# Second pass of the attention scores' main key blocks with 64 rows, two blocks in the two row halves of the array

## The chip, the cores and the metric

One core of one Trainium2 chip runs the whole layer as a single program. The metric is the device time of one execution in microseconds (us): 1670.31 us, the median of three runs (1669.04 to 1671.41). Rows of the trace come from one profiled execution. PE is TensorE, the matrix engine; PEld is its loading of weights, the operand that stays in the array; DVE is VectorE, ACT is ScalarE, POOL is GpSimd, and SP is the engine whose queue issues all transfers (DMAs).

## The reference, cut to what matters

One layer of a hybrid block: a normalised input is projected once, then a gated linear attention and a differential attention run on it, and both are merged, projected and added to the input. The change touches the scores of the differential attention alone: 8 heads, 1024 queries in 8 tiles of 128, 1280 keys (256 of the context, 1024 of the latents), and two components per head, each of width 64.

```
s1 = jnp.einsum('bhqd,bhkd->bhqk', qb1, k1).astype(jnp.float32) * scale
s2 = jnp.einsum('bhqd,bhkd->bhqk', qb2, k2).astype(jnp.float32) * scale
a = jax.nn.softmax(s1, axis=-1) - lam * jax.nn.softmax(s2, axis=-1)
return jnp.einsum('bhqk,bhkv->bhqv', a.astype(v.dtype), v)
```

## The kernel before

**Products in two parts.** The kernel works in float32 and has PE multiply in fp32r, a faster and less exact form. To keep the precision it splits an operand into a high part and a low part. Elsewhere a product takes three matmuls (high by high, high by low, low by high: `mm3`, line 359). For the scores the width is only 64, so both parts of the keys lie in one tile of 128 rows: `kk`, rows 0 to 63 the high part, rows 64 to 127 the low part (lines 1918 to 1920, two loads of 64 x 1280 from `d_kT[0]` and `d_kT[1]`). The query tile `aq` holds the same part of the queries in both row halves, index 0 the high part and index 1 the low part. So a first matmul over 128 rows gives high query by (high + low) key, and a second one adds low query by (high + low) key into the same place.

**One unit of scores** is one query tile of one head (`att_scores`, line 1957). Its output `s5` is one PSUM region of 2560 columns, 5 banks of 512. For each component two main blocks of 512 keys go to two banks of their own (`MAIN`, line 2050), and the remaining 256 keys of both components share the middle bank (`TAIL`, line 2049). Each block takes the two matmuls described above, so a unit is eight matmuls of 512 columns and four of 256, and there are 64 units. After a component's main blocks DVE takes the maximum over 1024 columns (`att_max`), ACT takes the exponential over 1280 columns out of PSUM (`att_exp`), DVE combines the two components (`att_mix`), PE transposes the result (`att_tr`; tiles `b` from `ident` and `e`), ACT and POOL split it into two parts, and PE multiplies it by the values (`att_av`; `b` from `at` and `vv`).

**What sets the order.** Every engine runs its instructions in the order written into the program. A planner (`Driver`, line 57) writes that order when the program is built: it keeps a clock for PE (`now`), prices every instruction by formulas (`mm`, line 353, prices a matmul of 512 columns at 0.009 + 512 x 0.000428 = 0.228 us), and lets the task with the highest priority go whose inputs are due by that clock. A `yield AtPE(0)` gives other tasks a turn. Between the attention's matmuls it places matmuls of the output gates and of the branch projections (`fill`, line 2215; tile `mb` from `h` and `wt`), spread over the units by `PACE` (line 2123). The last of them need the finished attention and come after it.

**Buffers of the keys.** `kk` has three buffers. A head uses two, the third already holds the first component of the next head, and the second component's load waits until the current head's last use of a buffer. SP issues transfers strictly in its own order, and waits for what a transfer needs.

Of the kernel before, what the change touches and what calls it, by code (L numbers as in the profile page):

```python
# [19 lines left out]
P = 128  # L20
# [3 lines left out]
T = S + CTX  # L24
# [221 lines left out]
class Hybrid:  # L246
# [22 lines left out]
        mm=("psA", 2), ma=("psA", 1), tp=("psA", 2), edge=("sbE", 1), gs=("psA1", 1), go=("psA1", 1), gt=("psA1", 1),  # L269
# [80 lines left out]
            yield  # L350
        self.d.spawn(later(), AtPE(at), prio=-9)

    def mm(self, out, lhsT, rhs, start, stop, more=False):
        self.ins = self.nc.tensor.matmul(out, lhsT, rhs, start=start, stop=stop, skip_group_check=more).ins  # L354
        n = rhs.free_size()
        c = 0.009 + max(n, 230) * 0.000428 if rhs.dtype == F32R else 0.006 + max(4 * n, 470) / 2400
        return self.d.op("PE", c, [out], [lhsT, rhs])

    def mm3(self, out, sh, sl, mh, ml, first, last, more=False):
        self.mm(out, sh, mh, first, False, more)  # L360
# [1544 lines left out]
    def att_keys(self):  # L1905

        yield self.ev_us
        for hd in range(8):
            c, x = hd // 4, hd % 4
            for i in range(10):  # L1910
                yield self.ev_st["dk", c, i]
            if hd:
                yield self.ev_q[0, 1]
            K = []
            for comp in range(2):
                rows = slice(64 * comp, 64 * comp + 64)
                yield from self.acq("kk")
                kt = self.t("kk", [P, T], F32R)
                self.dma(kt[0:64], self.d_kT[0][c][x, rows])
                self.dma(kt[64:128], self.d_kT[1][c][x, rows])  # L1920
                K.append(kt)
            self.K[hd] = K
            self.d.set(self.ev_k[hd], self.d.when(*K))
# [33 lines left out]
    def att_scores(self):  # L1957

        nc, d = self.nc, self.d
        yield self.ev_b  # L1960
        s5 = self.t("s5", [P, 2 * T])
        for hd in range(8):
            for qt in range(8):
                pr, qs = qt // 2, slice((qt % 2) * P, (qt % 2) * P + P)
                yield self.ev_k[hd]
                yield self.ev_q[hd, pr]
                K, Q = self.K[hd], self.Q[hd, pr]

                def score(po, comp, o, n):
                    bank = po.offset % (2 * T) // 512  # L1970
                    for j in range(2):
                        e = self.mm(po, Q[comp][:, j, qs], K[comp][:, o:o + n], j == 0, j == 1)
                        self.banked(self.ins, "PE", bank)
                    return e

                if qt % 4 == 0:
                    self.zs = self.t("sm", [P, 4, 2])
                u = dict(hd=hd, qt=qt, E=[None, None], mt=self.t("sm", [P, 2]), mx=[self.t("sm", [P, 1]) for _ in range(2)],
                         z=self.zs[:, qt % 4], zs=self.zs, left=2, min=[], ev=[Event() for _ in range(3)])

                for comp in range(2):
                    yield from self.acq(f"s{comp}")
                    pm = s5[:, 1536 * comp:1536 * comp + 1024]
                    for x, (o, n) in enumerate(self.MAIN[comp]):
                        e = score(pm[:, x * 512:(x + 1) * 512], comp, o, n)
                        if x == 0:
                            yield AtPE(0)
                    d.spawn(self.att_max(u, comp, s5, pm, 3 * comp, 3 * comp + 1), On(e, "DVE"), prio=-3)
                    yield AtPE(0)
                    if comp == 0:  # L1990
                        yield from self.acq("st")
                        pt = s5[:, 1024:1536].rearrange("p (c k) -> p c k", c=2)
                        for x in range(2):
                            e = score(pt[:, x], x, *self.TAIL[x])
                        d.spawn(self.att_max(u, 2, s5, pt, 2), On(e, "DVE"), prio=-3)
                    elif qt == 7:
                        self.rel("kk", e, 2)
                    yield AtPE(0)
                if qt % 2 == 1:
                    self.rel("aq", e, 2)  # L2000
                d.set(self.ev_u[8 * hd + qt])
# [47 lines left out]
    TAIL = ((1024, 256), (0, 256))  # L2049
    MAIN = (((0, 512), (512, 512)), ((256, 512), (768, 512)))  # L2050
    GROUPS = ((0, 4), (4, 4), (8, 2))

    def att_tr(self):

        d = self.d
        for hd in range(8):
            for qt in range(8):
                x = qt % 2
                yield self.ev_a[hd, qt]
                E = self.att[hd, qt][0]  # L2060
                if x == 0:
                    A = self.aT[hd, qt // 2] = []
                for g, (k0, n) in enumerate(self.GROUPS):
                    if x == 0:
                        tg = "at4" if n == 4 else "at2"
                        yield from self.acq(tg, 2)
                        A.append([self.t(tg, [P, n, 2, P], F32R) for _ in range(2)] + [tg])
                    if n == 2 and x == 0:
                        E0 = E
                        continue  # L2070
                    hi, lo = A[g][:2]
                    tb = "mc" if "psC" in self.pools else "b1"
                    yield from self.acq(tb)
                    if n == 4:
                        pt = self.t(tb, [P, n, P])
                        for j in range(n):
                            e = self.tr(pt[:, j], E[:, (k0 + j) * P:(k0 + j + 1) * P])
                        d.spawn(self.att_split(g, pt, hi[:, :, x], lo[:, :, x], [self.ev_aT[hd, qt, g]], tb), On(e, "ACT"), prio=self.PS)
                    else:
                        pt = self.t(tb, [P, 2, 2, P])  # L2080
                        for j in range(2):
                            for y, EE in enumerate((E0, E)):
                                e = self.tr(pt[:, j, y], EE[:, (k0 + j) * P:(k0 + j + 1) * P])
                        d.spawn(self.att_split(g, pt.rearrange("p a b t -> p (a b) t"), hi.rearrange("p a b t -> p (a b) t"),
                                               lo.rearrange("p a b t -> p (a b) t"),
                                               [self.ev_aT[hd, qt - y, g] for y in range(2)], tb), On(e, "ACT"), prio=self.PS)
                    yield AtPE(0)
                if x:
                    self.rel("e5", e, 2)

    def att_av(self):
        d = self.d
        for hd in range(8):
            for pr in range(4):
# [8 lines left out]
                VH, VL = self.V[hd]  # L2103
                for g, (k0, n) in enumerate(self.GROUPS):
                    hi, lo, tg = A[g]
# [583 lines left out]
```

## Time and profile before

| What | Value |
|---|---|
| median of three runs | 1670.31 us (1669.04 to 1671.41) |
| the profiled execution, its own time | 1671.82 us |
| its span, first to last instruction | 1670.1 us |
| PE busy | 1621.8 us, 97% of the span, 8317 matmuls |
| DVE busy | 1203.2 us, 72% |
| ACT busy | 832.1 us, 50% |
| POOL busy | 642.7 us, 38% |
| DMA | 178 GB/s on average |
| granted TensorE clock | 0.998 on average |

Matmuls overlap: the next one starts streaming while the one before still drains, so the recorded length of one is longer than the time it takes from the engine. The scores run from 970.7 us to about 1448 us of the span; after that come the end of the attention, the last branch projection and the output projection.

### The profile page before, as it was taken

How to read it: one execution, taken by the hardware profiler on the slowest of the kernel's cores; microseconds unless marked ns; L12 is line 12 of the kernel's file. 1: busy time of each engine (PE TensorE's matmuls, PEld its weight loads, DVE VectorE, ACT ScalarE, POOL GpSimd, SP SyncE). 2: the span in 40 equal slices, each digit the busy share in tenths (PEclk: the TensorE clock that was granted, in tenths of full speed). 3: DMA queues.
4: the chain of work that ended last, by engine and by line, in shares of the span. 5: the costliest groups of instructions: out<-in, count | busy, mean ns of one | idle time of the engine just before them, and what ended most of it. 6: DMA issues, size and time to landing. Idle time of an engine off the chain costs nothing.

```text
span 1670.1 us, 24453 instructions
## 1 busy us (share of the span) xinstructions
PE 1621.8 (97%) x8317; PEld 1344.4 (81%) x8317; DVE 1203.2 (72%) x1868; ACT 832.1 (50%) x1665; POOL 642.7 (38%) x619
## 2 busy tenths in 40 slices
PE   8999999999999999999999989999999999999999
PEld 3788888888788878888888778888888888878887
DVE  4675878878645475767777568897888888746694
ACT  4786568553523344442333346666666566642231
POOL 1600662643100113435454425555656566730000
PEclk9999999999999999999999999999999999999999
DMA  8646576455555464459999654443874534257422
GB/s 308 212 154 218 187 229 208 126 163 193 187 176 164 147 205 159 138 187 294 288 292 297 190 149 108 127 133 92 232 239 125 147 107 127 66 187 246 150 98 76
DMA packets 267005, 297.62 MB, mean 178 GB/s; under 512 B 23640, under 2 KB 186368, under 8 KB 266880
## 3 DMA queue, kind: packets, MB, share of 16 engines
q1 hardware_dynamic: 266880, 296.05, 56.8%
q8 instruction: 66, 1.08, 0.3%
q14 instruction: 59, 0.48, 0.1%
HBM read 196.37 MB, written 99.61 MB: 177 GB/s over the span
## 4 chain that ended last, share of the span: by engine, by line
PE 55%; DVE 10%; POOL 3%; issue 3%; ACT 3%; DMA 1%; SPq 0%; ACTq 0%; DVEq 0%; POOLq 0%
PE mc L354 10%; PE mm L354 7%; PE s L354 6%; PE mb L354 6%; PE b L354 5%; PE ma L354 5%; DVE sm L211 4%; PE go L354 3%; PE b L380 3%; PE gs L354 3%; PE gt L354 3%; PE tp L354 2%; DVE e L211 2%; ACT e L211 2%; POOL p L211 1%
## 5 line engine op out<-in xcount | busy, mean ns | idle before, releaser
L211 DVE TENSOR_REDUCE sm<-s 128x1 f32<-128x1024 f32 (+1 forms) x192 | 197.4, 1038 | 33.2 <-PE s L354 32.4
L354 PE MATMUL mm<-w,h 128*128 128x512 f32 x864 | 217.9, 400 | 3.3 <-DVE us L211 1.3
L211 ACT ACTIVATE e<-s,sm 128x1280 f32<-128x1280 f32 x128 | 170.1, 1331 | 86.4 <-DVE sm L211 78.3
L211 POOL TENSOR_TENSOR at<-ac,at 128x512 fp32r<-128x512 f32 x128 | 185.9, 1453 | 10.7
L354 PEld LDWEIGHTS mm<-w,h 128*128 128x128 f32 x864 | 158.8, 188 | 38.0 <-DVE us L211 1.7
L354 PE MATMUL s<-kk,aq 128*128 128x512 f32 (+1 forms) x768 | 174.1, 361 | 6.8 <-ACT e L211 6.8
L354 PE MATMUL mb<-h,wt 128*128 128x512 f32 x624 | 170.6, 404 | 6.1 <-DVE ft L211 3.6
L211 POOL TENSOR_SCALAR at<-ac 128x512 fp32r<-128x512 f32 x128 | 97.3, 760 | 188.5 <-ACT ac L211 183.2
L354 PE MATMUL mm<-h,w 128*128 128x512 f32 x624 | 154.1, 396 | 0.0
L354 PEld LDWEIGHTS s<-kk,aq 128*128 128x128 f32 x768 | 121.0, 188 | 26.3 <-ACT e L211 10.7
L354 PEld LDWEIGHTS mm<-h,w 128*128 128x128 f32 x624 | 115.6, 189 | 23.4 <-DVE h L211 0.2
L354 PE MATMUL b<-at,vv 128*128 128x256 f32 x960 | 129.7, 283 | 1.9 <-DVE at L211 1.5
L354 PEld LDWEIGHTS mb<-h,wt 128*128 128x128 f32 x624 | 109.6, 188 | 26.9 <-DVE ft L211 4.7
L354 PEld LDWEIGHTS b<-at,vv 128*128 128x128 f32 x960 | 120.9, 188 | 7.5 <-POOL at L211 2.7
L211 POOL TENSOR_TENSOR sm<-sm,nhalf 128x8 f32<-128x8 f32 (+3 forms) x78 | 103.1, 1322 | 30.9 <-DVE sm L211 25.6
L354 PE MATMUL mc<-h,wt 128*128 128x512 f32 x480 | 113.1, 396 | 1.6 <-DVE wt L211 1.6
L211 DVE SCALAR_TENSOR_TENSOR e<-e,sm,e 128x1280 f32<-128x1280 f32 x64 | 112.3, 1755 | 1.2
L354 PEld LDWEIGHTS mc<-h,wt 128*128 128x128 f32 x480 | 90.8, 190 | 22.3 <-DVE wt L211 2.5
L211 ACT ACTIVATE ac<-b 128x512 f32<-128x512 f32 x121 | 71.9, 598 | 57.3 <-PE b L380 55.0
L354 PE MATMUL ma<-w,h 128*128 128x512 f32 x384 | 96.8, 397 | 0.4 <-DVE gp L211 0.4
L380 PE MATMUL b<-ident,e 128*128 128x128 f32 x604 | 87.6, 273 | 6.8 <-DVE at L211 3.1
L380 PEld LDWEIGHTS b<-ident,e 128*128 128x128 f32 x604 | 72.5, 141 | 23.9 <-ACT ac L211 3.9
(385 smaller groups left out, 3170.2 us busy)
## 6 DMA issues: line engine op xcount, KB each, us to landing
raw<-in_w_in SPq DMA_DIRECT2D x37, 512.0 KB, 4.6
rb<-in_w_in SPq DMA_DIRECT2D x64, 256.0 KB, 2.9
aq<-d_qT SPq DMA_DIRECT2D x128, 128.0 KB, 4.0
d_kT<-pl SPq DMA_DIRECT2D x40, 256.0 KB, 2.4
d_dv<-pl SPq DMA_DIRECT2D x40, 256.0 KB, 2.3
kk<-d_kT SPq DMA_DIRECT2D x32, 320.0 KB, 5.2
gv<-d_v SPq DMA_DIRECT2D x40, 256.0 KB, 4.2
vv<-d_dv SPq DMA_DIRECT2D x16, 640.0 KB, 6.6
```

Of the source, the lines that this page charges most:

```text
L211: self.ins = f(out, *args, **kw).ins
L354: self.ins = self.nc.tensor.matmul(out, lhsT, rhs, start=start, stop=stop, skip_group_check=more).ins
L380: self.nc.tensor.transpose(out, src, self.ident[:n, :n])
```

## The change

In the second pass (low part of the queries) the two main blocks of a component are multiplied by the high part of the keys alone: 64 rows each instead of 128. The first block uses rows 0 to 63, the second block rows 64 to 127. So that both find the high part there, the halves of the key tile are swapped from the second block's first key on (`o`, 512 for the first component and 768 for the second): the load of a key tile becomes four transfers of 64 x 512 and 64 x 768 instead of two of 64 x 1280. What falls away is low query by low key in the main blocks. The four matmuls of a component now stand in the order first block high, second block high, first block low, second block low, without a turn for others between the blocks; the planner prices the two low ones at 0.1 and 0.23 us (`HALF`). The tail keeps both passes over 128 rows.

```diff
-    def mm(self, out, lhsT, rhs, start, stop, more=False):
+    def mm(self, out, lhsT, rhs, start, stop, more=False, cost=None):
...
-        return self.d.op("PE", c, [out], [lhsT, rhs])
+        return self.d.op("PE", cost or c, [out], [lhsT, rhs])
...
                 kt = self.t("kk", [P, T], F32R)
-                self.dma(kt[0:64], self.d_kT[0][c][x, rows])
-                self.dma(kt[64:128], self.d_kT[1][c][x, rows])
+                o = self.MAIN[comp][1][0]
+                for j, part in enumerate((slice(0, o), slice(o, T))):
+                    for hh in range(2):
+                        self.dma(kt[64 * hh:64 * hh + 64, part], self.d_kT[hh ^ j][c][x, rows, part])
...
-                def score(po, comp, o, n):
-                    bank = po.offset % (2 * T) // 512
-                    for j in range(2):
-                        e = self.mm(po, Q[comp][:, j, qs], K[comp][:, o:o + n], j == 0, j == 1)
-                        self.banked(self.ins, "PE", bank)
+                def score(po, comp, o, n, j, rows=slice(0, P), cost=None):
+                    e = self.mm(po, Q[comp][rows, j, qs], K[comp][rows, o:o + n], j == 0, j == 1, cost=cost)
+                    self.banked(self.ins, "PE", po.offset % (2 * T) // 512)
                     return e
...
                     for x, (o, n) in enumerate(self.MAIN[comp]):
-                        e = score(pm[:, x * 512:(x + 1) * 512], comp, o, n)
-                        if x == 0:
-                            yield AtPE(0)
+                        score(pm[:, x * 512:(x + 1) * 512], comp, o, n, 0)
+                    for x, (o, n) in enumerate(self.MAIN[comp]):
+                        e = score(pm[:, x * 512:(x + 1) * 512], comp, o, n, 1, slice(64 * x, 64 * x + 64), self.HALF[x])
...
                         for x in range(2):
-                            e = score(pt[:, x], x, *self.TAIL[x])
+                            for j in range(2):
+                                e = score(pt[:, x], x, *self.TAIL[x], j)
...
+    HALF = (0.1, 0.23)
```

On PE, one unit of the second head before. `s5` is the scores' region, `kk` a key tile, `aq` a query tile, `b1` a bank that takes transposes, `mb` a filler's bank; the size is that of the output, so the rows of the operands don't show here.

```order
L354 MATMUL s5_1958_9420<-kk_1939_9298,aq_2106_10105 128x512 x2
L380 MATMUL b1_2152_10305<-ident_207,ot_2108_10111 128x128 x2
L380 MATMUL b1_2152_10305<-ident_207,ot_2144_10286 128x128 x2
L354 MATMUL s5_1958_9420<-kk_1939_9298,aq_2106_10105 128x512 x2
L380 MATMUL b1_2153_10313<-ident_207,e5_2116_10136 128x128 x4
L354 MATMUL mb_2117_10138<-h0_150_640,wt_2046_9802 128x512
L354 MATMUL mb_2117_10138<-h0_151_641,wt_2046_9802 128x512
L354 MATMUL mb_2117_10138<-h0_150_640,wt_2047_9803 128x512
L354 MATMUL s5_1958_9420<-kk_1939_9298,aq_2106_10105 128x256 x2
L354 MATMUL s5_1958_9420<-kk_2072_9931,aq_2107_10108 128x256 x2
L354 MATMUL s5_1958_9420<-kk_2072_9931,aq_2107_10108 128x512 x4
```

The same unit of the same head after the change.

```order
L354 MATMUL s5_1956_9419<-kk_1939_9305,aq_2101_10082 128x512 x4
L354 MATMUL mb_2111_10131<-h0_150_640,wt_2043_9801 128x512
L354 MATMUL mb_2111_10131<-h0_151_641,wt_2043_9801 128x512
L354 MATMUL mb_2111_10131<-h0_150_640,wt_2044_9802 128x512
L354 MATMUL s5_1956_9419<-kk_1939_9305,aq_2101_10082 128x256 x2
L354 MATMUL s5_1956_9419<-kk_2058_9883,aq_2102_10085 128x256 x2
L354 MATMUL s5_1956_9419<-kk_2058_9883,aq_2102_10085 128x512 x4
L380 MATMUL b1_2154_10338<-ident_207,ot_2109_10127 128x128 x2
L380 MATMUL b1_2154_10338<-ident_207,ot_2149_10310 128x128 x2
```

The four matmuls of 512 columns always follow each other now (128 groups of four; before, 9 of the 128 had other work between the two blocks), and the other work in the unit has moved by a few rows; before the first key load, at PE's row 3208, the order is unchanged.

On SP, the key loads where the first head gives way to the second, before; `d_kT00` holds high parts, `d_kT10` low parts, and `d_m12` and `d_bT0` are other stores.

```order
L319 DMA d_m12_130<-ft_2045_9800 128x512
L319 DMA kk_2072_9931<-d_kT00_88 64x1280
L319 DMA kk_2072_9931<-d_kT10_90 64x1280
L319 DMA aq_2073_9934<-d_qT0_86 64x2x256 x2
L319 DMA aq_2074_9937<-d_qT0_86 64x2x256 x2
L319 DMA kk_2075_9940<-d_kT00_88 64x1280
L319 DMA kk_2075_9940<-d_kT10_90 64x1280
L319 DMA d_bT0_112<-b1k_2087_10013 128x512
```

The same place after the change.

```order
L319 DMA d_m12_130<-ft_2042_9799 128x512
L319 DMA kk_2058_9883<-d_kT00_88 64x768
L319 DMA kk_2058_9883<-d_kT10_90 64x768
L319 DMA kk_2058_9883<-d_kT10_90 64x512
L319 DMA kk_2058_9883<-d_kT00_88 64x512
L319 DMA aq_2059_9888<-d_qT0_86 64x2x256 x2
L319 DMA aq_2060_9891<-d_qT0_86 64x2x256 x2
L319 DMA kk_2061_9894<-d_kT00_88 64x512
L319 DMA kk_2061_9894<-d_kT10_90 64x512
L319 DMA kk_2061_9894<-d_kT10_90 64x768
L319 DMA kk_2061_9894<-d_kT00_88 64x768
```

Each key tile takes four issues instead of two, with the same bytes in all, and the query loads behind it stand two issues later.

## Rows read from the trace of the kernel before

**Rows 1.** Page, part 1: busy time, share of the span and instructions.
```profile
PE 1621.8 (97%) x8317; PEld 1344.4 (81%) x8317; DVE 1203.2 (72%) x1868; ACT 832.1 (50%) x1665; POOL 642.7 (38%) x619
```
**Rows 2.** Windows, scores and what follows: length, PE, PEld, DVE, ACT, POOL, clock, DMA.
```profile
970.70:1450.30 479.60, 460.40 (x2892) 400.74 (x2891) 406.93 (x614) 301.28 (x578) 284.01 (x251) 1.00 0.48 135
1450.30:1670.10 219.80, 213.42 (x997) 176.42 (x995) 140.24 (x213) 66.28 (x119) 22.65 (x21) 0.99 0.44 148
```
**Rows 3.** Chain that ended last, from 970 to 1450 us, shares by engine and line.
```profile
by line: PE s L354 21.7%; PE mb L354 16.4%; PE b L354 15.8%; DVE sm L211 12.3%; PE b L380 10.6%; DVE e L211 7.3%; ACT e L211 5.9%; issue 4.3%; DVE at L211 0.9%; POOL sm L211 0.8%; DVE b1k L211 0.8%; DMA aq<-d_qT 0.8%; ACT ac L211 0.8%; POOL
```
**Rows 4.** Waits, 970 to 1450 us: us in total, times, longest.
```profile
ACT e L211 <- DVE sm L211: 77.4, 51, 4.2
DVE sm L211 <- PE s L354: 32.4, 22, 13.4
PE s L354 <- ACT e L211: 6.8, 9, 2.8
PE mb L354 <- DVE ft L211: 3.6, 3, 1.8
PE b L380 <- DVE at L211: 3.1, 2, 1.5
```
**Rows 5.** Groups by shape, scores and transposes: busy, mean ns, idle before.
```profile
L354 PE MATMUL s<-kk,aq 128*128 128x512 f32 x512 | 143.6, 399 | 5.2 <-ACT e L211 5.2
L354 PE MATMUL s<-kk,aq 128*128 128x256 f32 x256 | 41.3, 283 | 1.6 <-ACT e L211 1.6
...
L380 PE MATMUL tp<-ident,p 128*128 128x128 f32 x144 | 21.9, 275 | 2.1 <-DVE p L211 1.1 <-POOL p L211 0.7
```
**Rows 6.** Chain in order of time: start, us, what; runs of 512 and 256 columns.
```profile
1027.50 2.83 PE b L354 x24
1612.03 21.76 PE mc L354 x96
```
**Rows 7.** Instructions on the scores' tile: duration ns min/median/max.
```profile
L354 PE MATMUL s<-kk,aq x768: 276/392/503, 970.7 to 1448.0; 128*128 128x512 f32 x128, 128*128 128x256 f32 x64
```
**Rows 8.** Timeline, PE and PEld near 24.6 us: two-row matmuls, then 128 rows.
```profile
24.41 0.40 PE L380 MATMUL gt<-ident,p 2*128 2x2 f32 x4 [0.63 <-DVE p L211]
24.62 0.20 PE L380 MATMUL gt<-ident,p 2*128 2x2 f32 x1
24.74 0.20 PEld L380 LDWEIGHTS tp<-ident,g 128*128 128x128 f32 x2
24.74 0.77 PE L380 MATMUL tp<-ident,g 128*128 128x128 f32 x5
24.91 0.14 PEld L380 LDWEIGHTS tp<-ident,g 128*128 128x128 f32 x1
```
**Rows 9.** Timeline, PE and PEld near 31.3 us: 128 columns of weights, then 4.
```profile
31.29 0.39 PE L354 MATMUL mm<-h,w 128*128 128x512 f32 x1
31.30 0.31 PEld L354 LDWEIGHTS gs<-w,cs 128*4 128x4 f32 x2
31.52 0.63 PE L354 MATMUL gs<-w,cs 128*4 128x512 f32 x2
```
**Rows 10.** DMA issues: count, KB each, median us to landing.
```profile
kk<-d_kT SPq DMA_DIRECT2D x32, 320.0 KB, 5.2
aq<-d_qT SPq DMA_DIRECT2D x128, 128.0 KB, 4.0
```
**Rows 11.** Timeline, SP's queue and PE where the second head ends.
```profile
1073.05 1.10 SPq L319 DMA_DIRECT2D kk<-d_kT  x2
1074.20 2.52 SPq L319 DMA_DIRECT2D aq<-d_qT  x4
1079.85 1.55 PE L354 MATMUL s<-kk,aq 128*128 128x512 f32 x8
```
**Rows 12.** Timeline, SP's queue before the linear attention.
```profile
761.70 0.45 SPq L319 DMA_DIRECT2D kk<-d_kT  x1
762.20 0.58 SPq L319 DMA_DIRECT2D bkt<-d_kt  x1
762.82 0.45 SPq L319 DMA_DIRECT2D gv<-d_v  x1
```

## The prediction

> **What bounds the kernel now.** I read the page's busy times first, then windows of the stage that changes, then the chain there, then the waits. PE is busy almost throughout, no other engine is [rows 1]; a busy PE is a modelled figure, so it only says where to look. In the stage of the scores, 479.6 us long, PE is the fullest engine and DVE the second with 406.9 us, 85% [rows 2]. So DVE would bound this stage only if it shrank by 73 us, far more than the change can take. The chain there runs through PE for about two thirds: the scores alone hold 21.7%, the fillers 16.4%, the products with the values 15.8%, the transposes 10.6%; DVE's maximum and mix and ACT's exponential hold 25.5% together [rows 3]. PE itself waits little: 6.8 us for the exponential that frees a scores' bank, 3.6 us and 3.1 us for DVE, while ACT and DVE wait for each other and for the scores far longer [rows 4]. The stage is therefore a full PE with about a third of the chain passing through the DVE and ACT loop. What follows is PE again: 213.4 of 219.8 us [rows 2], with the same fillers left over.
>
> **What a matmul takes.** A scores' matmul of 512 columns is recorded with 399 ns [rows 5], but they overlap. In a long run 96 matmuls of 512 columns take 21.76 us, so each takes 0.227 us from PE; 24 of 256 columns take 2.83 us, so 0.118 us [rows 6]. The scores thus take 512 x 0.227 + 256 x 0.118 = 146 us from PE.
>
> **The pair of half matmuls.** The change leaves the count at 12 matmuls per unit and makes four of them half as high. It makes 128 pairs (64 units, two components). A pair took 2 x 0.227 = 0.453 us. What it takes now no row of before shows: there is no matmul of 64 rows in this stage. The bounds:
> - Nothing is gained if the two run one after the other, each with all its columns: 0.453 us.
> - Everything is gained if they stream side by side: 0.227 us.
> - In between stands the weight load. Weights of a following matmul normally load while the one before streams, unseen. When they can't, the load shows: scores' matmuls have a median of 392 ns and a longest of 503 ns [rows 7], so an uncovered load of 128 columns costs 111 ns. The second half matmul's load stands behind the first half matmul in PE's order. If it starts only once that one has started, the second streams 0.111 us after the first, and the pair takes 0.111 + 0.227 = 0.338 us.
> I take the 0.338 us: the row that comes nearest is this load, and elsewhere a load begins when the matmul before it begins, not sooner (31.30 behind 31.29 us) [rows 9]. That saves 0.453 - 0.338 = 0.115 us a pair, 128 x 0.115 = 14.7 us of PE.
>
> The Trainium skill (TensorE: Matmul & The Clock Gate, Part 3) says that matmuls in distinct row groups start within 4 ns of each other, since the loads are pulled ahead. By that rule a pair would take 0.231 us. No row of before has two row groups, so it stays with the second rival.
>
> **What of it reaches the end.** The scores hold 21.7% of the chain over 480 us, so 104 us of their 146 us lie on it, 0.71. The rest of the time the chain passes through DVE and ACT, and a shorter matmul only lets PE wait longer. 14.7 x 0.71 = 10.5 us. What is late next is DVE's maximum of 1024 columns and ACT's exponential; both keep their lengths. The fillers don't run out: they are spread over the units, and those that are left after the scores are on PE anyway.
>
> **The key loads.** Sixteen key tiles take four issues instead of two, 32 more on SP. Two issues take 1.10 us [rows 11], so about 0.55 us each. Where a head ends, the second component's keys are issued at 1073.05 us and land 5.2 us after issue [rows 10], about 1078.8 us for the later one; the next head's scores start at 1079.85 us. The cover is 1 us. With four issues the last starts 1.1 us later; its piece is 128 or 192 KB instead of 320 KB, and query loads of 128 KB land in 4.0 us, so most of the delay comes back. I cost it at nothing. Without that cover it is at most 1.1 us at each of 7 changes of head, 7.7 us. Query loads stand behind them and are due two units later. Before the stage, the first head's keys stand ahead of loads for the linear attention [rows 12]; two more issues there are 0 to 1.1 us, I take 0.5.
>
> **The order.** Taking the turn between the blocks away costs nothing by itself, and only 9 of 128 groups had used it. But the planner's clock is 0.126 us shorter per pair, so from its first key load on the order of all engines is laid anew. A few matmuls of a filler more or less between two units is 0.7 us each time, in both directions; I count 0.5 us against the change and 3 us either way for the range.
>
> **Sum.** 10.5 - 0.5 - 0.5 = 9.5 us less. The profiled execution took 1671.82 us, 1.7 us more than its span, and 1.5 us more than the median; the same difference from the median 1670.31 gives 1660.8, so 1661 us.
>
> **Rivals.**
> - *The halves stream side by side.* The pair takes 0.227 us, PE saves 128 x 0.227 = 29 us, and at 0.71 and with the same 1 us against it the time is 1670.3 - 20.6 + 1 = 1651 us. For it: the operands lie in different rows and the results in different banks. Against it: a load starts with the matmul before it [rows 9].
> - *The change of height stops PE.* This is the one that makes it slower. Every pair needs two changes, from 128 rows to 64 and back. There is one place without a wait where matmuls of few rows are followed by 128 rows [rows 8]: four of two rows start 0.07 us apart, the last at 24.62 us, and the load for 128 rows starts only at 24.74 us, 0.12 us later, and it is seen: the next load starts at 24.91 us, 0.17 us after, where the remaining three of the five are (0.77 - 0.17 - 0.275) / 3 = 0.11 us apart (0.275 us is the mean length of such a transpose [rows 5]). Together 0.05 + 0.06 = 0.11 us lost. Twice that makes the pair 0.338 + 0.22 = 0.558 us, 0.105 us more than before, 13.4 us of PE; 0.71 to all of it on the path, with the 1 us, gives 1681 to 1685 us, 1683 us. It decides from 0.058 us a change on, half of the 0.115 us gained. The upper bound is that each change waits for the whole drain, 0.392 - 0.227 = 0.165 us, and then loads weights uncovered, 0.111 us: the pair takes 0.89 us, 128 x 0.437 = 56 us more, 1711 us at 0.71. Against it: weights of 4 columns follow 128 columns elsewhere, and the matmul starts 0.23 us later as always, with its load at the usual time [rows 9]; but there the rows stay the same.
> - *The halves run one after the other.* PE gains nothing, the order is laid for a gain that isn't there, and the loads cost their 1 us: 1670 to 1675 us, 1672 us. For it: each still streams 512 columns.
> - *The gain falls into the DVE and ACT loop.* If only 0.4 of the saved time reaches the end, 14.7 x 0.4 - 1 = 4.9 us are left, 1665 us. I count this within the forecast.
>
> The Trainium skill (TensorEngine Tiling (Array Packing), Key Properties) has a rule that speaks against the change: changing the tiling mode, not just the tile, drains the engine. The trace agrees by 0.11 us for a change in rows [rows 8], and shows no such loss for a change in columns [rows 9]. By the rule in full the time is that of the second rival's upper half.
>
> **Chances.** Forecast (0.338 us a pair) 0.42; side by side 0.14; stopped by the change of height 0.31; one after the other 0.13. The forecast's own range is 1655 to 1668 us: 0.4 to 0.9 of 14.7 us, less the 1 us, and 3 us either way for the order. The range of 8 in 10 reaches into both sides: 1651 us leaves out half of the side-by-side case, 0.07, and 1688 us leaves out a third of the stopped case, 0.11. A measurement tells about 0.2% (3.3 us) from no change. Faster by more: 0.40 of the forecast, all 0.14 of side by side, 0.01 of the rest: 0.55. Slower by more: 0.28 of the stopped case, 0.03 of one after the other: 0.31. Within: 0.14.
>
> **What the new profile would show.** Right: groups of 64 rows, 256 in all, the second of a pair starting about 0.11 us after the first and the next full matmul 0.23 us after that; the scores' stage some 10 us shorter with DVE's busy time in it unchanged at 407 us; PE's waits for the exponential a few us longer; the first scores of a head no later behind their key loads than the 6.8 us of now [rows 11]. Wrong: a gap of 0.1 us or more before the first half matmul or behind the second, with its weight load starting late (stopped); 0.227 us between the two (one after the other); nearly equal starts (side by side). If the pair takes 0.338 us and the time still doesn't fall by 6 us, the share of 0.71 was wrong; if SP's key loads end a wait of PE at the heads' ends, the cover of 1 us was.

## The result: 1690.5 us against 1670.9 us, slower by 1.2%

The changed kernel takes 1690.48 us (median of four runs, 1687.09 to 1693.42), the kernel before in the same session 1670.86 us (1669.04 to 1672.08). The ratio is 1.0118, its 95% interval 1.0096 to 1.014: 19.6 us lost where 9.5 us were to be won, and outside the range of 1651 to 1688 us. The profiled execution took 1689.76 us, with a span of 1688.0 us.

The page after, busy times; they answer to [rows 1].

```profile
PE 1642.5 (97%) x8317; PEld 1315.6 (78%) x8317; DVE 1204.6 (71%) x1867; ACT 831.4 (49%) x1665; POOL 641.3 (38%) x620
```

PE has as many instructions as before and 21 us more of (modelled) busy time; the busy time of its weight loads is 29 us less. A load of 64 rows is about as long as one of 128 (185 and 191 ns on average), but the two loads of a pair run at the same time, so 256 of them fill only 24.1 us. Every other engine does what it did.

The instructions on the scores' tile after: minimum, median and longest duration in ns, then the first and the last start in us; this answers to [rows 7].

```profile
L354 PE MATMUL s<-kk,aq x768: 275/397/794, 968.0 to 1468.4; 128*128 128x512 f32 x128, 128*128 128x256 f32 x64
```

The scores now take 500.4 us from first to last start, 23.1 us more than the 477.3 us before. They begin 2.7 us earlier and what follows them is 2.5 us shorter, so the stage holds the whole loss.

The chain that ended last, after, from 970 to 1450 us, for [rows 3].

```profile
by line: PE s L354 25.5%; PE mb L354 21.3%; PE b L354 20.1%; PE b L380 13.9%; DVE sm L211 5.4%; ACT e L211 2.6%; DVE e L211 2.3%; issue 1.8%; DMA aq<-d_qT 1.6%; POOL at L211 1.1%; DVE b1k L211 0.8%; DMA raw<-in_w_br_gla 0.8%; ACT ac L211 0.
```

PE's four lines hold 81% of it instead of 64.5%; DVE and ACT have fallen back. So PE became slower, and nobody else's waits took its place. The scores' groups by shape, 960 to 1480 us, for [rows 5] (busy us, mean ns of one, idle us just before them and what ended it), and two waits of the stage for [rows 4].

```profile
L354 PE MATMUL s<-kk,aq 128*128 128x512 f32 x256 | 83.5, 408 | 6.9 <-ACT e L211 6.9
...
L354 PE MATMUL s<-kk,aq 64*128 64x512 f32 x256 | 64.8, 503 | 0.0
...
L354 PEld LDWEIGHTS s<-kk,aq 64*128 64x128 f32 x256 | 24.1, 185 | 47.1 <-issue 47.1
```

```profile
PEld s L354 <- issue: 46.8, 131, 0.7
...
PE s L354 <- ACT e L211: 7.3, 8, 2.5
```

A half matmul is recorded with 503 ns on average, the length of a matmul whose weight load is not covered (before, the longest was 503 ns [rows 7]), and the loads for it stood idle 47.1 us with nothing in the trace to wait for. The timeline shows one pair: PE's matmuls and PEld's loads in order of start (start us, length us; in brackets the idle time before).

```profile
1037.88 0.39 PE L354 MATMUL s<-kk,aq 128*128 128x512 f32 x1
1038.10 0.40 PE L354 MATMUL s<-kk,aq 128*128 128x512 f32 x1
1038.43 0.19 PEld L354 LDWEIGHTS s<-kk,aq 64*128 64x128 f32 x2 [0.36 <-issue]
1038.43 0.50 PE L354 MATMUL s<-kk,aq 64*128 64x512 f32 x2
1038.86 0.30 PEld L354 LDWEIGHTS b<-at,vv 128*128 128x128 f32 x2 [0.25 <-issue]
1038.86 0.39 PE L354 MATMUL b<-at,vv 128*128 128x256 f32 x1
```

Both loads of the pair start 0.33 us behind the second full matmul, where the load before had started together with a matmul; the two half matmuls lie in one row of 0.50 us, that is, on top of each other; the next load, of 128 rows, again starts only 0.43 us later. Over the 128 pairs the medians of the starts are: from the second full matmul to the first half one 326 ns, to the second half one 3 ns, to what follows 429 ns. With full rows in the same order (the first experiment) each of the three is 232 ns. What follows is then seen with its own load as well: a matmul takes 107 to 114 ns more than with full rows (65 pairs), a transpose 56 ns more (63 pairs). Row by row against full rows, a pair loses 0.17 us of PE with a matmul behind it and 0.12 us with a transpose behind it, 18.7 us in all. The expectations below reckon 0.184 us behind every pair, 23.6 us; they count a matmul's load there each time and 0.227 us for a distance that is 0.232 us here, so they are some 5 us too high.

The key loads, for [rows 10] and [rows 11]: the issues by size (count, KB, median us to landing), and four of them in SP's queue.

```profile
kk<-d_kT SPq DMA_DIRECT2D x32, 192.0 KB, 3.4
kk<-d_kT SPq DMA_DIRECT2D x32, 128.0 KB, 3.6
```

```profile
1079.64 2.38 SPq L319 DMA_DIRECT2D kk<-d_kT  x4
```

Four issues take 2.38 us, 0.6 us each, and their pieces land 1.6 to 1.8 us sooner than the whole did.

### The profile page after: what moved, and what is told of

It reads as the page before. It is cut to its first block, busy times and chain, and to the rows that moved or that the text cites. A ratio compares the mean times of both kernels' runs of the same rounds, so it can differ in the third digit from the quotient of the medians.

```text
span 1688.0 us, 24504 instructions
## 1 busy us (share of the span) xinstructions
PE 1642.5 (97%) x8317; PEld 1315.6 (78%) x8317; DVE 1204.6 (71%) x1867; ACT 831.4 (49%) x1665; POOL 641.3 (38%) x620
## 4 chain that ended last, share of the span: by engine, by line
PE 62%; DVE 6%; POOL 3%; issue 2%; ACT 2%; DMA 2%; SPq 0%; ACTq 0%; DVEq 0%; POOLq 0%
PE mc L354 9%; PE mb L354 8%; PE mm L354 8%; PE s L354 8%; PE b L354 6%; PE ma L354 5%; PE b L380 4%; PE go L354 3%; PE gs L354 3%; PE gt L354 3%; PE tp L354 2%; DVE sm L211 2%; POOL p L211 1%; PE mz L354 1%; DVE w L211 1%
## 5 line engine op out<-in xcount | busy, mean ns | idle before, releaser
L354 PE MATMUL s<-kk,aq 128*128 128x512 f32 (+2 forms) x768 | 173.2, 401 | 7.5 <-ACT e L211 7.3
L354 PEld LDWEIGHTS s<-kk,aq 128*128 128x128 f32 (+1 forms) x768 | 97.8, 189 | 64.8 <-issue 49.5
L211 POOL TENSOR_TENSOR sm<-sm,nhalf 128x8 f32<-128x8 f32 (+3 forms) x78 | 99.1, 1270 | 22.0 <-DVE sm L211 14.9
L380 PE MATMUL b<-ident,e 128*128 128x128 f32 x604 | 91.5, 283 | 3.9 <-ACT ac L211 3.0
L380 PEld LDWEIGHTS b<-ident,e 128*128 128x128 f32 x604 | 68.9, 143 | 25.6 <-issue 12.9
```

The source lines that it names most:

```text
L211: self.ins = f(out, *args, **kw).ins
L380: self.nc.tensor.transpose(out, src, self.ident[:n, :n])
```

## The experiments

My theory after the result: PE stops at every change of height, 256 times. The rivals: the order that the planner laid for prices that aren't true, and the doubled key loads. Ratios are to the kernel before, run on the same chip in the same session, with 95% intervals.

**The change without its heights.** In the changed kernel the second pass gets all 128 rows; loads, prices and the row order of every engine stay.

```diff
-  e = score(..., o, n, 1, slice(64 * x, 64 * x + 64), self.HALF[x])
+  e = score(..., o, n, 1, slice(0, P), self.HALF[x])
```

> The changed kernel with the second pass of the main blocks over all 128 rows again; key loads, swapped halves and the order of every engine are those of the changed kernel. Theory (the change of height stops PE): the changed trace shows the first half matmul 0.326 us behind the full one before it where 0.227 is usual, the second 3 ns after the first, the next matmul 0.429 us later, and 0.107 us more before the one after that: 0.865 us where four full ones take 0.681, so 0.184 us a pair, 23.6 us of PE for 128 pairs, of which 19.6 of the 19.6 us measured. Without heights the time falls back to 1668 to 1675 us. Rival 1 (the order laid for too short prices costs it): the order is unchanged, so the time stays at 1685 to 1692 us. Rival 2 (the doubled key loads on SP): also 1685 to 1692 us.

Measured 1681.58 us (1677.07 to 1682.64), ratio 1.0053 (1.004 to 1.0067). Neither fits: the heights are a good half of the loss, 0.65%, and 0.53% stay without them. The chain from 970 to 1450 us is back where it was before; PE's four lines hold 65%:

```profile
by line: PE s L354 22.9%; PE b L354 16.7%; PE mb L354 16.1%; DVE sm L211 12.2%; PE b L380 9.6%; DVE e L211 5.7%; ACT e L211 4.5%; issue 3.0%; POOL at L211 2.2%; DMA aq<-d_qT 1.6%; DVE at L211 1.2%; DVE b1k L211 1.1%; ACT ac L211 1.1%; DVE f
```

Part of the 0.53% goes with the clock that TensorE was granted, a share of its full speed, averaged over an execution: at 0.998 and 0.997 this kernel took 1677.07 and 1678.2 us, at 0.995 and 0.994 1681.18 to 1682.64 us; the kernel before, in the same session, took 1670.79 to 1673.84 us at 0.998. At the same clock some 3 to 6 us are left of the 9. The heights' share hardly depends on it: the changed kernel took 1687.09 us at 0.998 and 1693.42 us at 0.994, 10 to 11 us more than this run at either.

**Both halves in the same rows.** No swap of the keys' halves, both half matmuls in rows 0 to 63; order as in the changed kernel.

```diff
-  self.dma(kt[...], self.d_kT[hh ^ j][c][x, rows, part])
+  self.dma(kt[...], self.d_kT[hh][c][x, rows, part])
-  slice(64 * x, 64 * x + 64)
+  slice(0, 64)
```

> The changed kernel with both half matmuls in rows 0 to 63, and the keys' halves not swapped (still four loads a tile); the order of every engine is that of the changed kernel. The changes of height are the same in number, but the two halves share their rows. Theory: the stops stay as they are and the second half matmul streams behind the first, 0.227 us later instead of 3 ns, with no stop between them: 128 x 0.224 = 28.7 us of PE more than the changed kernel, 1712 to 1722 us. Rival (the stop comes from using both row groups at once, not from the height): the stops vanish, and the time is that of four full matmuls, 1668 to 1676 us. Rival (order): 1688 to 1695 us.

Measured 1718.77 us (1713.95 to 1723.35), ratio 1.0282 (1.0258 to 1.0305), as the theory had it: 1.64% above the changed kernel, 27.4 us. The timeline of one pair:

```profile
1045.60 0.50 PE L354 MATMUL s<-kk,aq 64*128 64x512 f32 x1
1045.60 0.29 PEld L354 LDWEIGHTS s<-kk,aq 64*128 64x128 f32 x2 [0.37 <-issue]
1045.94 0.40 PE L354 MATMUL s<-kk,aq 64*128 64x512 f32 x1
```

The second one is 0.40 us long, the usual length: its load ran behind the first and isn't seen. So a stop comes with the change of height, not with every half matmul, and not from using two row halves. That the two halves overlap in the change is worth these 27 us, of which some 3 go with the clock: two of the four executions had 0.991 (1722.93 and 1723.35 us), the other two, at 0.995 and 0.996, took 1713.95 and 1714.6 us, 23 to 24 us more than the changed kernel at the same clock.

**Half the pairs.** Half matmuls for the second component alone.

```diff
+  slice(64 * x, 64 * x + 64) if comp else slice(0, P)
```

> The changed kernel with half matmuls for the second component alone: 64 pairs instead of 128; the first component's second pass has 128 rows; order of every engine and loads as in the changed kernel. Theory (each pair costs 0.184 us of PE): half the loss, 1677 to 1684 us. Rival (order or loads): 1686 to 1692 us. Rival (only the first component's pairs, which free the bank that DVE waits for first, matter): 1668 to 1675 us.

Measured 1684.55 us (1680.95 to 1685.99), ratio 1.0075 (1.0062 to 1.0087). This lies between the theory's range and the rival's, 0.55 us above the first. The time rises with the number of pairs: 0.53%, 0.75%, 1.18% for 0, 64 and 128 of them, the second 64 costing more than the first.

**True prices.** The changed kernel, laid anew with what the trace shows.

```diff
-    HALF = (0.1, 0.23)
+    HALF = (0.2, 0.437)
```

> The changed kernel with the planner's prices for the two half matmuls at what the trace shows, 0.2 and 0.437 us instead of 0.1 and 0.23: the order is laid anew, the matmuls are the same. Theory (the stops are PE time that no order gives back): 1686 to 1693 us, the same as the changed kernel within 0.3%. Rival (the mispriced order is most of the loss): 1672 to 1681 us.

Measured 1690.51 us (1689.57 to 1692.14), ratio 1.0115 (1.0101 to 1.013): the same. The true prices alone don't bring the time back. Since the order was laid anew as well, and the experiments further down show that a new order costs by itself, this run doesn't say what the wrong prices cost.

**What the other half per cent is.** Three runs with full rows, each laid anew by the planner: the change with full rows at a true price; the kernel before with the four key loads alone; the kernel before with the new order of the four matmuls alone.

```diff
-  e = score(..., 1, slice(64 * x, 64 * x + 64), self.HALF[x])
+  e = score(..., 1)
```

> As the run with full rows in the changed order, but the planner prices the second pass at 0.228 us, what a full matmul takes, so the order of all engines is laid anew; key loads in four parts, both high matmuls ahead of both low ones, no turn between the blocks. That run kept 0.53% over the kernel before, about 9 us, without any change of height. Theory A (its order was laid for PE time that isn't there): 1668 to 1674 us. Rival B (the four key loads) and rival C (the order of the four matmuls without a turn): 1676 to 1683 us.

```diff
-  self.dma(kt[0:64], self.d_kT[0][c][x, rows])
-  self.dma(kt[64:128], self.d_kT[1][c][x, rows])
+  (the four loads of the change)
```

> The kernel before with the key loads in four parts and the halves swapped, and nothing else. A: 1668 to 1674 us, as before (the cover of 1 us at the heads' ends holds). B: 1676 to 1683 us. C: as before.

```diff
+  (the four matmuls in the order of the change, 128 rows, no turn between the blocks; two key loads)
```

> The kernel before with the four matmuls of a component in the order high, high, low, low, full rows, no turn between the blocks, true price, and the two key loads of before. A and B: 1668 to 1674 us. C: 1676 to 1683 us.

Measured 1683.49 us, ratio 1.0078 (1.0065 to 1.009); 1681.05 us, 1.0064 (1.0052 to 1.0077); 1676.89 us, 1.0042 (1.0029 to 1.0056). All three lose, and the parts don't add up (0.64% and 0.42% apart, 0.78% together): that points at what they have in common, an order laid anew.

**Fewer changes of height.** The half matmuls of both components behind the second component's high ones, so 128 changes instead of 256.

```diff
+  for comp in range(2): (both high matmuls; after the first component the tail)
+  for comp in range(2):
+      for x, (o, n) in enumerate(self.MAIN[comp]):
+          e = score(..., comp, o, n, 1, slice(64 * x, 64 * x + 64), self.HALF[comp][x])
+  HALF = ((0.2, 0.23), (0.005, 0.43))
```

> The changed kernel with the half matmuls of both components put together behind the second component's high ones: 4 half matmuls in a row, so two changes of height a unit instead of four (128 instead of 256), at the same 128 pairs; the planner prices them at 0.2, 0.23, 0.005, 0.43 us. The first component's maximum comes later by the tail and two matmuls, about 0.9 us. Theory (the cost is per change of height, about 0.205 us each, and a pair streams side by side for 0.227 us less): PE gives back 128 x 0.205 = 26 us of the changed kernel's 23.6 us loss, 2.8 us less PE than before; with the later maximum 1668 to 1682 us. In the trace the third half matmul starts 0.23 us behind the first pair with its weights loaded in time. Rival (the cost is per pair of row groups): still 0.18 us a pair, 1688 to 1700 us.

Measured 1692.41 us (1690.11 to 1696.83), ratio 1.0136 (1.0121 to 1.0151). The time missed my range and lies in the rival's; the trace speaks for the theory. PE's matmuls at one unit:

```profile
1043.90 0.40 PE L354 MATMUL s<-kk,aq 128*128 128x512 f32 x1
1044.22 0.50 PE L354 MATMUL s<-kk,aq 64*128 64x512 f32 x2
1044.57 0.40 PE L354 MATMUL s<-kk,aq 64*128 64x512 f32 x2
1044.89 0.39 PE L354 MATMUL b<-at,vv 128*128 128x256 f32 x1
```

The first pair has the stop before it and the long 0.50 us; the second pair follows with 0.40 us, loads covered; then the stop again. So the price is per change of height, and PE's busy time is 1627.4 us, 15 us less than the changed kernel's. What most likely ate the gain stands in this kernel's waits, 970 to 1470 us:

```profile
DVE sm L211 <- ACT e L211: 57.2, 47, 2.3
...
PEld s L354 <- ACT e L211: 24.7, 36, 2.6
```

The same two waits in the changed kernel are 22.8 and 10.9 us: the first component's maximum and exponential come later, and the bank that the next unit needs comes free later. I had put the delay at 0.9 us a unit and no more. No run takes the delay away and keeps the rest, so this reading is argued, not shown.

**Loads or order, apart.** The planner's account and the loads themselves can be parted. First four loads, while the planner reckons two: PE, DVE, ACT and POOL keep the order of before row for row. Then the reverse: two loads, while the planner reckons four.

```diff
+  self.nc.sync.dma_start(...)      (four times: the parts of the change)
+  self.d.dma(4 * 64 * T, ...)      (the planner's account: twice)
```

> The kernel before with the key loads in four parts and the halves swapped, while the planner reckons two loads as before: PE, DVE, ACT and POOL keep the order of before row for row, SP issues 32 more loads. With the planner told of the four loads the kernel before had become 0.64% slower. Theory A (the order laid anew costs it): 1668 to 1674 us. Theory B (the loads themselves cost it, at the heads' ends or in front of the linear attention): 1677 to 1684 us.

```diff
+  self.nc.sync.dma_start(...)      (twice: whole halves)
+  self.d.dma(4 * 64 * n, ...)      (the planner's account: four times)
```

> The reverse: two loads a key tile as before, while the planner reckons four, so PE, DVE, ACT and POOL have row for row the order of the run with four loads alone. Theory A (order): 1677 to 1684 us. Theory B (loads): 1667 to 1674 us.

Measured 1670.49 us, ratio 0.9994 (0.9985 to 1.0002), and 1679.78 us, ratio 1.0045 (1.0032 to 1.0058). The loads cost nothing; the order costs 0.45%, 7.5 us, with the very loads and matmuls of before. Its scores last from 967.3 to 1458.4 us, 13.8 us longer, and PE waits more for the exponential that frees a scores' bank, here from 960 to 1470 us, against 6.8 us in 9 waits before [rows 4].

```profile
PE s L354 <- ACT e L211: 11.9, 14, 2.7
```

The waits are the smaller part of it. Windows of the scores before and in this order, and four pieces of the latter (length, busy time of PE, PEld, DVE, ACT, POOL, granted clock, DMA):

```profile
970.70:1448.00 477.30, 458.11 (x2875) 398.76 (x2874) 404.66 (x610) 300.68 (x577) 281.90 (x250) 1.00 0.48 135
967.00:1458.40 491.40, 468.35 (x2880) 403.23 (x2879) 403.56 (x611) 300.40 (x578) 289.34 (x250) 0.99 0.48 133
973.00:976.40 3.40, 3.40 (x11) 2.55 (x10) 2.64 (x6) 1.07 (x4) 0.00 (x0) 0.50 0.27 78
1252.80:1256.30 3.50, 3.50 (x12) 2.72 (x11) 0.47 (x1) 0.00 (x0) 1.67 (x2) 0.51 0.74 180
1317.70:1321.10 3.40, 3.40 (x11) 2.62 (x10) 2.24 (x3) 0.00 (x0) 3.32 (x3) 0.50 0.52 173
1444.00:1447.40 3.40, 2.92 (x9) 2.43 (x10) 2.33 (x6) 0.91 (x3) 1.90 (x2) 0.50 0.20 77
```

PE's idle time in the stage grew by 4 us, its busy time by 10 us with nearly the same number of matmuls. In the four pieces, 13.7 us together, the granted clock was at the lower of its two levels, 1.2 GHz; at most half of that, 6.8 us, is lost by it, and the stage before had no such piece. This trace is of an execution at a mean clock of 0.994. At 0.998 three executions took 1677.47 to 1679.78 us, against 1670.26 to 1672.6 us before: at the same clock the order still costs about 6 us.

**The heights in the order of before.** Both with four loads reckoned as two, high matmuls first, the turn for others kept in the middle and full prices, so the row order is that of before; the first with 64 rows in the second pass, the second with 128.

```diff
   for x, (o, n) in enumerate(self.MAIN[comp]):
       e = score(pm[:, x * 512:(x + 1) * 512], comp, o, n, 0)
   yield AtPE(0)
   for x, (o, n) in enumerate(self.MAIN[comp]):
-      e = score(pm[:, x * 512:(x + 1) * 512], comp, o, n, 1, slice(64 * x, 64 * x + 64))
+      e = score(pm[:, x * 512:(x + 1) * 512], comp, o, n, 1, slice(0, P))
```

> The change's half matmuls in the order of before: four loads reckoned as two, both high matmuls first, the turn for others kept in the middle of the four, full prices, so the other engines and PE's row order are those of before; only the second pass has 64 rows in two row halves. Theory (a change of height costs 0.2 us of PE, 0.184 us a pair net): 23.6 us more PE, of which 0.5 to 0.85 reach the end: 1682 to 1691 us. Rival (the loss of the change was its order and loads): 1668 to 1676 us.

> The same with 128 rows in the second pass: it differs from that run in the heights alone, and from the kernel before in four loads instead of two and in the order of the four matmuls of a group. Theory A: 1668 to 1674 us. Theory B: 1677 to 1684 us. If the order of the four matmuls costs by itself, 1673 to 1678 us.

Measured 1682.75 us (1682.07 to 1684.46), ratio 1.0066 (1.0053 to 1.0078), with 64 rows, and 1670.36 us (1668.15 to 1673.13), ratio 0.9991 (0.9982 to 1.0), with 128. The heights alone cost 12.4 us. The scores' matmuls of the first and of the second, first and last start:

```profile
L354 PE MATMUL s<-kk,aq x768: 276/397/793, 968.8 to 1461.6; 128*128 128x512 f32 x128, 128*128 128x256 f32 x64
```

```profile
L354 PE MATMUL s<-kk,aq x768: 276/392/792, 970.0 to 1449.7; 128*128 128x512 f32 x128, 128*128 128x256 f32 x64
```

492.8 us against 479.7 us: the difference lies in the stage. Windows of the two, between these starts, with the same granted clock:

```profile
968.80:1461.60 492.80, 479.29 (x2876) 369.29 (x2874) 404.62 (x611) 300.73 (x577) 275.48 (x250) 0.99 0.45 131
970.00:1449.70 479.70, 461.24 (x2876) 401.19 (x2875) 405.03 (x611) 301.18 (x577) 282.61 (x250) 0.99 0.46 135
```

PE is busy 18.1 us longer and the stage lasts 13.1 us longer; the missing 5 us are idle time of PE that got shorter (18.5 to 13.5 us).

**Is the order of before a picked one?** Three kernels with matmuls, loads and arithmetic of before, and one of the planner's prices moved a little: a transfer's issue 0.46 us instead of 0.45, an fp32r matmul 1 ns dearer, a transpose 1 ns dearer. In the second and the third the planner also gives a few of DVE's instructions to POOL, which then has 623 and 626 instead of 619.

```diff
-  t = max(...) + 0.45
+  t = max(...) + 0.46
```

> The kernel before with the planner's price for issuing a transfer at 0.46 instead of 0.45 us; instructions are the same, their order differs in part. Theory (the order of before is a picked one, and any other loses): 1675 to 1683 us. Rival (only what the change told the planner makes a worse order): 1668 to 1674 us.

```diff
-  c = 0.009 + max(n, 230) * 0.000428
+  c = 0.010 + max(n, 230) * 0.000428
```

> The kernel before with the planner's price of an fp32r matmul 1 ns higher; instructions are the same, their order differs. Theory (picked order): 1675 to 1683 us. Rival: 1668 to 1674 us.

```diff
-  return self.d.op("PE", 0.109, [out], [src])
+  return self.d.op("PE", 0.110, [out], [src])
```

> The kernel before with the planner's price of a transpose 1 ns higher; instructions are the same, their order differs. Theory (picked order): 1675 to 1683 us. Rival: 1668 to 1674 us.

Measured 1672.41 us, ratio 1.0001 (0.9992 to 1.001); 1693.94 us, ratio 1.0131 (1.0117 to 1.0144); 1673.23 us, ratio 1.001 (1.0001 to 1.0018). Neither theory holds for all three. A nanosecond on one price can cost 22 us, more than the whole change, or next to nothing: in these runs the order laid anew is a draw between 0 and 1.3%. None of the seven orders with full rows that were tried was faster than the one of before. The clock has a part here too: the four executions of the dear one had 0.992 to 0.994, and the kernel before at its lowest there, 0.995, took 1673.43 us, so most of the 22 us is not the clock. The third ran at up to 1.0, and at 0.999 took 1672.34 to 1673.23 us against 1669.5 to 1671.29 us before: its order loses some 3 us that the median hides. The dear one:

```profile
L354 PE MATMUL s<-kk,aq x768: 275/392/632, 980.3 to 1471.5; 128*128 128x512 f32 x128, 128*128 128x256 f32 x64
```

Its scores begin 9.6 us later than before and last 491.2 us, 13.9 us longer: the loss arises in the stages ahead as well as in this one. Which rows of an order make it good stays open.

## Why the prediction was wrong

The step that failed first is "I take the 0.338 us": I let the second half matmul wait for its weights and let the changes of height cost nothing.

- *PE bounds the stage*: right, and more so after.
- *The pair*: it streams side by side, 3 ns apart, as the first rival had it; the load that I put between the two (0.111 us) lies in front of both, which start loading 3 ns apart. The Trainium skill (TensorE: Matmul & The Clock Gate, Part 3) had said within 4 ns for distinct row groups, and the trace agrees. (The prediction leaves that rule with "the second rival"; it is the first.)
- *The change of height*: the second rival's mechanism. It had 0.11 us a change, from matmuls of two columns that were followed by transposes. Measured, against 0.232 us with full rows in the same order: from the start of the second full matmul to the streaming of the half ones 0.326 + 0.108 (503 - 395 ns) = 0.434 us, so 0.202 us lost; on the way back 0.429 - 0.108 + 0.107 = 0.428 us, 0.196 us lost with a matmul behind, and 0.145 us with a transpose, whose load shows with 56 ns. That [rows 8] has transposes behind is one reason why it gave less. About half of a change is the load that can't run ahead, half the idle time before it, which [rows 8] had shown and I gave a chance of 0.31. The Trainium skill (TensorEngine Tiling (Array Packing), Key Properties) has it that changing the tiling mode drains the engine; the trace agrees, with 0.2 us a change in this kernel. What [rows 9] showed, no cost at a change of columns, doesn't carry over to rows.
- *Both rivals hold at once*, and I had priced each as if the other were false: 0.229 us saved, 0.40 us paid (0.35 with a transpose behind), net 0.17 us lost a pair (0.12). That the second rival's 1683 us comes close to the 1682.75 us of the heights alone is luck: it had the pair 0.11 us too dear and each change about 0.09 us too cheap.
- *The share of 0.71*: about right. Of the 18.1 us that PE lost, 12.4 us reached the end in the order of before, 0.69. The rest filled waits that PE had anyway. With both halves in the same rows a further 30 us or so of PE cost 27.4 us, 23 to 24 us at the same clock: PE's four lines hold 92% of the chain there, so few waits are left to fill.
- *The key loads*: nothing, as costed (ratio 0.9994); the cover of 1 us held.
- *The order*: I counted 0.5 us and 3 us either way. It costs 7.5 us with old loads, about 6 us at the same clock, and a nudge showed up to 22 us. This term was mis-sized even if the first had been right: a gain of 9.5 us is inside what a new order can take away.

The sum in the changed kernel's own order: 0.53% for the order and its clock, 0.65% for the heights, 1.18% or 19.6 us. The two terms that were measured apart, 12.4 us for the heights in the order of before and 7.5 us for an order laid for four loads, add up to 19.9 us; since that order is not the changed kernel's, how close this comes is partly chance.

## What to carry to other kernels

Halving the rows of a matmul can pay only if enough of them stand together: here each way in and out cost up to 0.2 us, and one pair saved 0.229 us, so one pair between full matmuls loses. That more pairs together gain is an estimate from these numbers; the one run with two pairs together gained no time. Where a planner lays the order, run the edit with the old order and the new order with the old work; without the two, 7.5 us of a draw would have been put down to the edit. Compare executions at the same granted clock before a few us are put down to an order. When a row and a rival disagree with the row you prefer, price them together, not each alone.

## What the runs showed of the hardware

A matmul of 64 rows behind one of 64 rows has its weights loaded in time, whether in the same rows (340 ns from the first's start to the second's, the first's own load of 108 ns included) or in the other half (3 ns). Of what was tried here, only a change between 64 and 128 rows stopped the loading.

The granted clock of TensorE fell twice in the scores after: from 985.9 us on, 6.8 us at 0.53, the lower level of 1.2 GHz, and at 1454 us for a shorter time. PE had waited 2.33 us for an exponential just before the first and 1.58 us for DVE just before the second. Windows and timeline:

```profile
985.90:992.70 6.80, 5.97 (x23) 4.55 (x24) 6.24 (x9) 2.83 (x6) 3.04 (x3) 0.53 0.18 58
992.70:1450.00 457.30, 444.47 (x2694) 343.53 (x2693) 374.69 (x561) 278.27 (x537) 264.01 (x235) 1.00 0.45 133
1453.50:1458.00 4.50, 4.50 (x17) 3.13 (x18) 1.81 (x3) 0.61 (x2) 2.82 (x3) 0.62 0.44 144
```

```profile
985.11 1.16 PE L354 MATMUL s<-kk,aq 128*128 128x512 f32 x4 [2.33 <-ACT e L211]
1453.47 1.25 PE L354 MATMUL mb<-h,wt 128*128 128x512 f32 x3 [1.58 <-DVE ft L211]
```

That is about 5 us of the profiled execution at most (3.2 and 1.7 us, by the share that was missing). At the place of the first, the clock fell in three kernels with half matmuls in this order: the changed one, the one with half the pairs (from 983.8 us on, 6.8 us at 0.50) and the one with both halves in the same rows (from 986.4 us on, 10.2 us at 0.50). With full rows in the same order PE waited 2.18 us there and the clock stayed at 1.00. Half matmuls are not needed for a fall: the order laid for four loads has four such pieces with full rows. Why the clock fell at one wait and not at another stays open.
